# A hybrid decoder trunk on one core: a one-step mask, later conditioning products, a reordered last MLP and a last norm on VectorE

## The chip, the core and the metric

The kernel runs on one core of one Trainium2 chip. Five engines work side by side and are tied by semaphores: PE (TensorE, matrix products; PEld is its weight load), DVE (VectorE), ACT (ScalarE), POOL (GpSimd) and SP (SyncE, which here issues most transfers). SBUF is the on-chip memory, PSUM holds TensorE's sums. The metric is the device time of one execution in microseconds (us), smaller is better.

## The reference

One sequence of 256 tokens, width 1024, float32 throughout, two layers. Each layer is a mixer and an MLP, each one conditioned by shift, scale and gate computed from a vector `c`, and each closed by a layer norm.

```python
for layer in range(2):
    shift, scale, gate = ada_modulation(c, ada_w[layer, 0], ada_b[layer, 0])   # silu(c) @ w + b; 1.0 + gate
    h = x * (1.0 + scale) + shift
    y = mixer_ab(h, ...) if layer % 2 == 0 else mixer_c(h, ...)
    x = layer_norm(DN_ALPHA * x + gate * y, ln_g[layer, 0], ln_b[layer, 0])
    shift, scale, gate = ada_modulation(c, ada_w[layer, 1], ada_b[layer, 1])
    h = x * (1.0 + scale) + shift
    y = jnp.square(jax.nn.relu(h @ w1[layer])) @ w2[layer]                      # 1024 -> 4096 -> 1024
    x = layer_norm(DN_ALPHA * x + gate * y, ln_g[layer, 1], ln_b[layer, 1])
```

`mixer_ab` (layer 0) has eight heads of sliding-window attention (A) and eight heads of sparse attention (B). In B an indexer scores all earlier tokens, each query keeps the 64 with the highest scores (`lax.top_k`), and the softmax runs over these picks alone. `mixer_c` (layer 1) is block-sparse attention whose block is as long as the sequence.

## The kernel before

The 256 tokens are two blocks of 128, one token per partition; they are called block 0 and block 1. A float32 product is made of three products (lines 251 to 253): each operand is split into a high part, a cast on ScalarE (line 174), and a low part, the subtraction of that cast on VectorE or, for the weight `wo` of the mixer's output, on GpSimd (line 175). Weights come in pieces of 1 MB through four buffers that are used in turn, so that a new transfer starts when an old piece has been read.

The order on each engine comes from a list scheduler. It takes instructions in the order of the code, shifted by `later(...)` and a table `LATER` of hand-set numbers. `behind(what, m)` adds one order between two instructions: `m` comes after the instruction that was put in `state[what]` last.

The change touches four places.

*The picks of B (`select`, lines 838 to 857).* VectorE takes eight maxima eight times (lines 852, 853) and overwrites each picked score with the number `SENT`. Two instructions then make the mask: line 856 writes `NEG` (a huge negative number) where the score is not `SENT` and 0 where it is, line 857 adds the causal mask `m`. Block 0 has 128 scores per row, block 1 has 256.

*The conditioning products (`ada_product`, line 337).* A product of `c` with a 128 x 1024 piece of the conditioning weights is one VectorE instruction. Two pieces, with keys ("ada", 1, 6) and ("ada", 1, 7), that is `w_ada_1_6` and `w_ada_1_7` in the order below, are late: two products each, so four in all. They belong to the shift and the scale of layer 0's MLP. `facA` and `facB` (lines 410 to 414) are made from them.

*The attention of B (`half_step`).* TensorE makes scores (`ps_s`, line 548), VectorE their row minimum of the negated scores (`negm`, line 552), ScalarE the exponential (line 556), TensorE transposes and the product with the values (line 570), VectorE the division (lines 584, 586). In the same stretch TensorE makes the output product of the mixer (`ps_out`) into two accumulators that are used in turn, the conditioning rows (`ps_ada`, line 362), and a broadcast of the gate (line 433) from rows that ScalarE casts (line 428). `residual` (line 625) multiplies a finished accumulator by the gate and so frees it.

*The last MLP and the last norm.* The MLP goes in 16 chunks of 256 hidden columns. `first(i)` is a chunk's first layer with the activation, `second(i, b, h)` its six products into one of four accumulators (block b, half h of the 1024 columns). `finish(b, zst)` makes a block's last products and its two residuals. `held` is true for layer 0 alone: there block 1's products of chunks 13 and 14 already stand behind block 0's. The last norm of block 0 is split: 672 columns on ScalarE and GpSimd, then 352 (`beside_vector`, lines 1132 to 1143); that of block 1 is on VectorE (lines 1153 and 1155). The reciprocal root `rs` of every norm is made on GpSimd (line 317).

Of the kernel before, what the change touches and what calls it, by code (L numbers as in the profile page):

```python
# [21 lines left out]
AF = mybir.ActivationFunctionType  # L22
ALU = mybir.AluOpType

P = 128
D = 1024
KT = 8
NB = 2
# [1 line left out]
ALPHA = 4 ** 0.25  # L30
LN_EPS = 1e-5
RMS_EPS = 1e-6
NEG = -1e30
SENT = -3e38
BIG = 3e38
NTOP = 64
IW_SCALE = 8 ** -0.5 * 64 ** -0.5
# [30 lines left out]
def trunk(ctx: ExitStack, tc, c, x, pos, small, ln, ada, w_g, w_g1, w_uq, w_out, c_in, c_out, w1, w2, out):  # L68
    nc = tc.nc
# [19 lines left out]
    def col(shape, name, bufs=4, dtype=F32):  # L89
        return work.tile(shape, dtype, name=name, tag=name, bufs=bufs)  # L90
# [178 lines left out]
    xt = []  # L269
# [12 lines left out]
    for h in range(2):  # L282
        ps = pa("ps_c")
# [49 lines left out]
    def ada_product(key, j, w):  # L333

        junk = work.tile([P, D], BF16, name="junk", tag="junk", bufs=1)
        m, bias = ada_bias(key, j)
        state[key, j] = nc.vector.tensor_tensor_reduce(out=junk, in0=w, in1=cB, scale=1.0, scalar=bias,  # L337
                                                       op0=ALU.mult, op1=ALU.add, accum_out=m)
        if j == 1:
            ada_factors(key)  # L340
        return 1 - j

    def behind(what, m):

        if what in state:
            tc.add_manual_dep(m.ins, state[what].ins.name, mybir.DependencyInfo(
                mybir.DependencyClass.NoSync, mybir.DependencyReason.DATA))
# [49 lines left out]
    done = set()  # L397
# [140 lines left out]
    def drain():  # L538
        while pipe:
            advance()  # L540
# [47 lines left out]
    def together(*gens):  # L588

        gens = list(gens)  # L590
        while gens:
            for g in list(gens):
                if next(g, gens) is gens:
                    gens.remove(g)
# [24 lines left out]
    def new_z():  # L619
        return work.tile([P, D], F32, name="z", tag="w4", bufs=2), col([P, 2, 6], "stats")  # L620

    def residual(b, h, ps, gB, zst, what=None):
        z, st = zst
        s = slice(h * 512, (h + 1) * 512)
        behind(what, nc.vector.tensor_mul(z[:, s], ps, gB[:, s]))
        nc.vector.scalar_tensor_tensor(z[:, s], in0=xt[b][:, s], scalar=ALPHA, in1=z[:, s], op0=ALU.mult, op1=ALU.add)
        nc.vector.bn_stats(st[:, h], z[:, s])

    def moments(st):
        mv = col([P, 2], "mv")  # L630
# [120 lines left out]
    for b in range(NB):  # L751
# [9 lines left out]
        ps = pc("ps_cq")  # L761
# [84 lines left out]
    def select(b, sc):  # L846

        nk = P * (b + 1)
        m = mC[:, P:] if b == 0 else mC
        for r in range(NTOP // 8):  # L850
            mx = col([P, 8], "mx")
            nc.vector.max(out=mx, in_=sc[:, :nk])
            nc.vector.match_replace(out=sc[:, :nk], in_to_replace=mx, in_values=sc[:, :nk], imm_value=SENT)
            if r % 2 and r < NTOP // 8 - 1:
                yield
        nc.vector.tensor_scalar(sc[:, :nk], sc[:, :nk], -2e38, NEG, op0=ALU.is_gt, op1=ALU.mult)
        nc.vector.tensor_add(mB[:, b, :nk], sc[:, :nk], m)


    ys = [work.tile([P, D], F32, name=f"y{b}", tag="w4", bufs=2) for b in range(NB)]  # L860
# [51 lines left out]
    def mixed_out(ys, name, i, first, second, under_first, under_second, after):  # L912
# [43 lines left out]
        def go(todo):  # L956
            for group in todo.split("|"):
                for s in group.split():
                    step(s)
                yield  # L960

        together(first, go(under_first))
        together(second, go(under_second))
        drain()
        together(go(after))

# [12 lines left out]
    def mlp(l, hT, rest, rows):  # L979
# [43 lines left out]
        def second(i, b, h):  # L1023
            halves = need(("w2", l, i))
            for f in range(2):
                s = slice(f * 256 + b * P, f * 256 + (b + 1) * P)
                wh, wl = halves[f]
                o = slice(h * 512, (h + 1) * 512)
                for m in mm3(acc[b][h], (us[i][0][:, s], us[i][1][:, s]), (wh[:, o], wl[:, o]),
                             i == 0 and f == 0, i == 15 and f == 1):  # L1030
                    if held and (i > 13 or b and i == 13):
                        behind("last", m)
                        state["last"] = m

# [6 lines left out]
        for i in range(16):  # L1041
            if i >= 1:
                need(("w2", l, i - 1))
            if held and i == 15:
                need(("w2", l, i))
                ahead(2)
            if i > 1:
                first(i)
            if held and i == 15:
                for cast, low in firsts:  # L1050
                    behind("cast", cast)
                    behind("vector", low)
            if i == at:
                gB, gb = rows()
            for _ in range(steps.get(i, 0)):
                next(more)
            if i < 15:
                need(("w1", l, i + 1))
            if 1 <= i < 15:
                for b in range(NB):  # L1060
                    for h in range(2):
                        if not (held and b and i == 14):
                            second(i - 1, b, h)
        need(("w2", l, 15))

        def finish(b, zst):
            if held and b:
                for h in range(2):
                    second(13, b, h)
            if held:  # L1070
                for h in range(2):
                    second(14, b, h)
            for h in range(2):
                for i in (15,) if held else (14, 15):
                    second(i, b, h)
                residual(b, h, acc[b][h], gB, zst, "norm" if held and b else None)

        return finish, gb

# [47 lines left out]

    finish, gb = mlp(1, hT, rest, lambda: (gate_row(3), ln_rows(3)))
    zs = [new_z() for b in range(NB)]
    halves = [slice(0, 512), slice(512, D)]  # L1130

    def beside_vector(b, s, mv, rs, after=None):

        nb = col([P, 1], "nb")
        z = zs[b][0]
        nc.vector.scalar_tensor_tensor(nb, in0=mv[:, 0:1], scalar=-1.0, in1=rs, op0=ALU.mult, op1=ALU.mult)
        nc.scalar.activation(z[:, s], z[:, s], AF.Identity, bias=nb, scale=rs)
        m = nc.gpsimd.tensor_mul(xt[b][:, s], z[:, s], gb[0][:, s])
        if after:
            tc.add_manual_dep(m.ins, after.ins.name, mybir.DependencyInfo(  # L1140
                mybir.DependencyClass.NoSync, mybir.DependencyReason.DATA))
        nc.gpsimd.tensor_add(xt[b][:, s], xt[b][:, s], gb[1][:, s])
        (nc.scalar if after else nc.sync).dma_start(out[b * P:(b + 1) * P, s], xt[b][:, s])

    finish(0, zs[0])
    first = moments(zs[0][1])
    beside_vector(0, slice(0, 672), *first)
    finish(1, zs[1])
    mv, rs = moments(zs[1][1])
    beside_vector(0, slice(672, D), *first, after=state["pow"])  # L1150
    for s in halves:
        z = zs[1][0]
        nc.vector.scalar_tensor_tensor(z[:, s], in0=z[:, s], scalar=mv[:, 0:1], in1=gb[0][:, s],  # L1153
                                       op0=ALU.subtract, op1=ALU.mult)
        nc.vector.scalar_tensor_tensor(xt[1][:, s], in0=z[:, s], scalar=rs, in1=gb[1][:, s], op0=ALU.mult, op1=ALU.add)  # L1155
        nc.sync.dma_start(out[P:, s], xt[1][:, s])


def _ktiles(w, cols):
# [50 lines left out]
```

## Time and profile before

| | us |
|---|---|
| three runs | 658.65, 658.56, 656.78 |
| median | 658.56 |
| the profiled execution | 659.22 |
| its span | 657.4 |
| PE busy | 629.9 (96%) |
| DVE busy | 472.9 (72%) |
| ACT busy | 337.9 (51%) |
| POOL busy | 55.9 (9%) |

Its mean granted TensorE clock is 0.987. The span starts with the first recorded instruction and ends with the last; 1.8 us of the profiled execution lie outside it. A row of the timeline has the start in us from the span's start, the duration in us, the engine, the line, the operation, what it writes and reads with partitions x elements, a count, and in brackets the engine's idle time before it with what ended it. DMA share is the busy share of the core's 16 transfer engines.

### The profile page before, as it was taken

The numbers are of one execution on the slowest core, as the hardware profiler recorded it, in microseconds if no ns is written. First come the engines' busy times: TensorE is split into PE (matmuls) and PEld (weight loads), VectorE is DVE, ScalarE is ACT, GpSimd is POOL, SyncE is SP. The second block draws the span as 40 slices with busy tenths as digits, with TensorE's granted clock in tenths as the row PEclk, the third lists the DMA queues.
The fourth block names the chain that finished last, engine by engine and source line by source line (L and its number), as shares of the span: only waits on it lengthen the run. The fifth ranks groups of instructions, "written<-read, shape, count | busy, mean of one in ns | idle before, by whom it ended". The sixth has DMA issues, their size and how long they took to land. (4 is left out here: it accounts for less than half of the span.)

```text
span 657.4 us, 9765 instructions
## 1 busy us (share of the span) xinstructions
PE 629.9 (96%) x3762; PEld 529.9 (81%) x3762; DVE 472.9 (72%) x858; ACT 337.9 (51%) x536; POOL 55.9 (9%) x77
## 2 busy tenths in 40 slices
PE   6998998999999999999989999999999999999993
PEld 3555686878898989898877888888889899998982
DVE  2948997677788879986987985745877755553447
ACT  3315666465555445545645446855564545455440
POOL 5010147000010000200011000000000000000004
PEclk9999998999999999999989999999999999999997
DMA  8992796435789997999833683501567745665101
GB/s 311 409 415 92 279 349 257 187 128 172 276 295 331 364 348 262 373 335 372 326 129 128 231 338 137 192 1 64 192 230 274 275 182 192 223 226 192 65 0 64
DMA packets 24384, 151.50 MB, mean 230 GB/s; under 512 B 2833, under 2 KB 3089, under 8 KB 8338
## 3 DMA queue, kind: packets, MB, share of 16 engines
q1 hardware_dynamic: 24194, 150.71, 62.9%
q8 instruction: 29, 0.48, 0.3%
q10 hardware_dynamic: 144, 0.18, 0.1%
q14 instruction: 17, 0.14, 0.1%
HBM read 149.83 MB, written 1.05 MB: 229 GB/s over the span
## 5 line engine op out<-in xcount | busy, mean ns | idle before, releaser
L175 DVE TENSOR_TENSOR wl<-w_w,wh 128x1024 fp32r<-128x1024 f32 x128 | 153.5, 1222 | 76.4 <-ACT wh L174 76.2
L174 ACT CAST wh<-w_w 128x1024 fp32r<-128x1024 f32 x128 | 131.0, 1050 | 147.1 <-PE ps_m L252 67.0
L251 PE MATMUL ps_m<-hTh,wh 128*128 128x256 f32 x448 | 126.7, 283 | 0.0
L253 PE MATMUL ps_m<-hTh,wl 128*128 128x256 f32 x448 | 126.6, 283 | 0.0
L252 PE MATMUL ps_m<-hTl,wh 128*128 128x256 f32 x448 | 126.6, 283 | 0.0
L337 DVE CUSTOM_DVE_ANT_0 junk<-w_ada,cB,sm 128x1024 bf16<-128x1024 f32 x72 | 95.7, 1328 | 9.3 <-DMA w_ada<-in_ada_dram 7.9
L251 PE MATMUL ps_m<-wh,uh 128*128 128x512 f32 x256 | 101.5, 397 | 0.0
L253 PE MATMUL ps_m<-wh,ul 128*128 128x512 f32 x256 | 101.5, 397 | 0.0
L252 PE MATMUL ps_m<-wl,uh 128*128 128x512 f32 x256 | 101.0, 395 | 0.0
L252 PEld LDWEIGHTS ps_m<-hTl,wh 128*128 128x128 f32 x448 | 85.7, 191 | 1.3
L251 PEld LDWEIGHTS ps_m<-hTh,wh 128*128 128x128 f32 x448 | 85.7, 191 | 1.2
L253 PEld LDWEIGHTS ps_m<-hTh,wl 128*128 128x128 f32 x448 | 85.7, 191 | 0.1
L253 PEld LDWEIGHTS ps_m<-wh,ul 128*128 128x128 f32 x256 | 48.2, 188 | 11.3 <-DVE ul L175 0.2
L251 PEld LDWEIGHTS ps_m<-wh,uh 128*128 128x128 f32 x256 | 48.3, 189 | 10.1 <-ACT uh L174 0.3
L252 PEld LDWEIGHTS ps_m<-wl,uh 128*128 128x128 f32 x256 | 48.2, 188 | 9.7
L251 PE MATMUL ps_c<-wh,hTh 128*128 128x512 f32 x96 | 38.7, 406 | 2.1 <-ACT hTh L174 2.1
L252 PE MATMUL ps_c<-wl,hTh 128*128 128x512 f32 x96 | 38.7, 405 | 0.0
L253 PE MATMUL ps_c<-wh,hTl 128*128 128x512 f32 x96 | 38.0, 399 | 0.0
L556 ACT ACTIVATE prob<-prob,negm 128x128 f32<-128x128 f32 (+1 forms) x64 | 26.7, 451 | 18.7 <-DVE negm L552 18.7
L317 POOL TENSOR_TENSOR rs<-rs,mhalf 128x1 f32<-128x1 f32 x8 | 7.6, 944 | 330.2 <-DVE rs L633 330.2
L175 DVE TENSOR_TENSOR ul<-relu,uh 128x512 fp32r<-128x512 f32 (+1 forms) x36 | 22.6, 629 | 16.6 <-ACT uh L174 16.6
L175 DVE TENSOR_TENSOR wl<-w_ci,wh 128x1024 fp32r<-128x1024 f32 x24 | 28.8, 1221 | 5.6 <-ACT wh L174 5.6
(231 smaller groups left out, 1016.8 us busy)
## 6 DMA issues: line engine op xcount, KB each, us to landing
w_w<-in_w_dram SPq DMA_DIRECT2D x64, 1024.0 KB, 5.1
w_ada<-in_ada_dram SPq DMA_DIRECT2D x40, 1024.0 KB, 7.0
w_ci<-in_c_in_dram SPq DMA_DIRECT2D x12, 1024.0 KB, 5.7
w_ada<-in_ada_dram SPq DMA_DIRECT2D x12, 512.0 KB, 9.5
w_wo<-in_w_out_dram SPq DMA_DIRECT2D x4, 1024.0 KB, 6.0
w_co<-in_c_out_dram SPq DMA_DIRECT2D x4, 1024.0 KB, 5.1
w_g<-in_w_g_dram SPq DMA_DIRECT2D x8, 356.0 KB, 9.0
early<-in_ada_dram SPq DMA_DIRECT2D x4, 512.0 KB, 9.2
```

What stands on the lines that cost most here:

```text
L174: state["cast"] = nc.scalar.copy(dh, src)
L175: return eng.tensor_sub(dl, src, dh.bitcast(F32))
L251: return [nc.tensor.matmul(ps, a[0], b[0], start=start, stop=False), nc.tensor.matmul(ps, a[0], b[1], start=False, stop=False), nc.tensor. ...
L252: nc.tensor.matmul(ps, a[0], b[1], start=False, stop=False),
L253: nc.tensor.matmul(ps, a[1], b[0], start=False, stop=stop)]
L317: state["pow"] = nc.gpsimd.tensor_tensor(out=dst, in0=src, in1=mhalf, op=ALU.pow)
L337: state[key, j] = nc.vector.tensor_tensor_reduce(out=junk, in0=w, in1=cB, scale=1.0, scalar=bias, op0=ALU.mult, op1=ALU.add, accum_out=m)
L556: state["exp"] = nc.scalar.activation(pr[:, j, :nk], pr[:, j, :nk], AF.Exp, bias=negm[:, hd:hd + 1], scale=-1.0)
```

## The change

It has four parts.

- **A.** The two mask instructions become one, (m + SENT) − score, with `SENT` = −2e38 and `NEG` = −1e38. For a pick the score is `SENT`, and the result is the causal mask.
- **B.** The four late conditioning products are collected in `lates` and put behind the last row minimum that was recorded, the last one of block 1 in B.
- **C.** In the last MLP block 1's products of chunks 13 and 14 now also stand behind block 0's, and the first residual multiply of each half behind the statistics of the half before.
- **D.** Both blocks' last norm is on VectorE, block 0's result in pieces of 512 and 512 columns, block 1's in 512, 256 and 256, each sent off on SP's or ScalarE's queue in turn.

```diff
-NEG = -1e30
-SENT = -3e38
+NEG = -1e38
+SENT = -2e38
...
+        if key[0] == "ada" and key[1:] in ((1, 6), (1, 7)):
+            lates.append(state[key, j])
...
-    def residual(b, h, ps, gB, zst, what=None):
+    def residual(b, h, ps, gB, zst):
...
-        behind(what, nc.vector.tensor_mul(z[:, s], ps, gB[:, s]))
+        m = nc.vector.tensor_mul(z[:, s], ps, gB[:, s])
...
-        nc.vector.bn_stats(st[:, h], z[:, s])
+        return m, nc.vector.bn_stats(st[:, h], z[:, s])
...
-        nc.vector.tensor_scalar(sc[:, :nk], sc[:, :nk], -2e38, NEG, op0=ALU.is_gt, op1=ALU.mult)
-        nc.vector.tensor_add(mB[:, b, :nk], sc[:, :nk], m)
+        nc.vector.scalar_tensor_tensor(mB[:, b, :nk], in0=m, scalar=SENT, in1=sc[:, :nk], op0=ALU.add, op1=ALU.subtract)
...
+        while lates:
+            behind("least", lates.pop())
         drain()
...
-                    if held and (i > 13 or b and i == 13):
+                    if i > 13 or b and i == 13:
                         behind("last", m)
...
-                        if not (held and b and i == 14):
+                        if not (b and i == 14):
                             second(i - 1, b, h)
...
         def finish(b, zst):
-            if held and b:
+            for i in range(14 - b, 15) if held or not b else ():
                 for h in range(2):
-                    second(13, b, h)
-            if held:
-                for h in range(2):
-                    second(14, b, h)
+                    second(i, b, h)
             for h in range(2):
-                for i in (15,) if held else (14, 15):
+                for i in range(13, 16) if b and not held else (15,):
                     second(i, b, h)
-                residual(b, h, acc[b][h], gB, zst, "norm" if held and b else None)
+                m, done = residual(b, h, acc[b][h], gB, zst)
+                behind("norm" if held and b else None if held else "done", m)
+                state["done"] = done
...
-    finish(0, zs[0])
-    first = moments(zs[0][1])
-    beside_vector(0, slice(0, 672), *first)
-    finish(1, zs[1])
-    mv, rs = moments(zs[1][1])
-    beside_vector(0, slice(672, D), *first, after=state["pow"])
-    for s in halves:
-        z = zs[1][0]
-        nc.vector.scalar_tensor_tensor(z[:, s], in0=z[:, s], scalar=mv[:, 0:1], in1=gb[0][:, s],
-                                       op0=ALU.subtract, op1=ALU.mult)
-        nc.vector.scalar_tensor_tensor(xt[1][:, s], in0=z[:, s], scalar=rs, in1=gb[1][:, s], op0=ALU.mult, op1=ALU.add)
-        nc.sync.dma_start(out[P:, s], xt[1][:, s])
+        mv, rs = moments(zs[b][1])
+        for s in (slice(0, 512), slice(512, D)):
+            nc.vector.scalar_tensor_tensor(z[:, s], in0=z[:, s], scalar=mv[:, 0:1], in1=gb[0][:, s],
+                                           op0=ALU.subtract, op1=ALU.mult)
+        cuts = (0, 512, 768, D) if b else (0, 512, D)
+        for q, lo, hi in zip((nc.sync, nc.scalar, nc.sync), cuts, cuts[1:]):
+            nc.vector.scalar_tensor_tensor(xt[b][:, lo:hi], in0=z[:, lo:hi], scalar=rs, in1=gb[1][:, lo:hi],
+                                           op0=ALU.mult, op1=ALU.add)
+            q.dma_start(out[b * P:(b + 1) * P, lo:hi], xt[b][:, lo:hi])
```

What moves on the engines is seen best in their order. Lines of the changed kernel are counted anew: its 556, 588, 590 and 629 are 552, 584, 586 and 625 before. On VectorE, before, in block 1's attention of B, from the second row minimum of a pair to the first of the next pair (the numbers behind the names are the buffers'; `junk` is the discarded product of line 337, `mod1_170` its sum; `w_ada_1_6` and `w_ada_1_7` are the two late pieces; a row with one name reads out the sum or the minimum of the row ahead of it):

```order
L552 ISA prob_1137,negm_1134<-ps_s_1136,pair_370 128x256
L552 ISA negm_1134 128x1
L584 RECIPROCAL den_1151<-ps_pv_926 128x4
L337 ISA junk_1209,mod1_170<-w_ada_1_6_977,cB_123,sm_75 128x1024
L337 ISA mod1_170 128x1
L586 TENSOR_TENSOR y0_444<-ps_pv_926,den_1151 128x2x2x64
L337 ISA junk_1236,mod1_170<-w_ada_1_7_1024,cB_123,sm_75 128x1024
L337 ISA mod1_170 128x1
L552 ISA prob_1193,negm_1134<-ps_s_1192,pair_370 128x256
L552 ISA negm_1134 128x1
```

And now, behind the last row minimum of block 1, where no product stands between the minima (`yTl` is the low part of the transposed attention output, `z` the first residual):

```order
L337 ISA junk_1162,mod1_170<-w_ada_1_6_976,cB_123,sm_75 128x1024
L337 ISA mod1_170 128x1
L175 TENSOR_TENSOR yTl_985<-evac_1241,yTh_984 128x512
L588 RECIPROCAL den_1299<-ps_pv_1133 128x4
L337 ISA junk_1207,mod1_170<-w_ada_1_6_976,cB_123,sm_75 128x1024
L337 ISA mod1_170 128x1
L590 TENSOR_TENSOR y1_445<-ps_pv_1133,den_1299 128x2x2x64
L337 ISA junk_1234,mod1_170<-w_ada_1_7_1023,cB_123,sm_75 128x1024
L337 ISA mod1_170 128x1
L629 TENSOR_TENSOR z_1245<-ps_out_1079,gateB_1177 128x512
L337 ISA junk_1281,mod1_170<-w_ada_1_7_1023,cB_123,sm_75 128x1024
```

The four products have left the stretch between the row minima, and three of them stand between the last minimum and the first residual multiply; the fourth follows that multiply.

On TensorE, before, where chunk 15's first layer (`ps_m1_6075`) begins in the last MLP; the accumulators `ps_m2_4481` and `ps_m2_4482` are block 0's halves, `ps_m2_4483` and `ps_m2_4484` block 1's:

```order
L253 MATMUL ps_m2_4484<-wh_5979,ul_5932 128x512
L251 MATMUL ps_m2_4484<-wh_5983,uh_5931 128x512
L252 MATMUL ps_m2_4484<-wl_5984,uh_5931 128x512
L253 MATMUL ps_m2_4484<-wh_5983,ul_5932 128x512
L251 MATMUL ps_m1_6075<-hTh_4455,wh_5971 128x256
```

And now, where the names are two lower: `ps_m2_4479` and `ps_m2_4480` are block 0's, and `ps_m1_6061` is chunk 15's first layer:

```order
L253 MATMUL ps_m2_4480<-wh_5977,ul_5930 128x512
L251 MATMUL ps_m2_4480<-wh_5981,uh_5929 128x512
L252 MATMUL ps_m2_4480<-wl_5982,uh_5929 128x512
L253 MATMUL ps_m2_4480<-wh_5981,ul_5930 128x512
L251 MATMUL ps_m1_6061<-hTh_4453,wh_5969 128x256
```

Chunk 15's first layer now follows block 0's products of chunk 13, and block 1's twelve products of that chunk have moved behind it, to the end.

On VectorE, the end of the kernel before:

```order
L633 TENSOR_SCALAR rs_6175<-mv_6173 128x1
L625 TENSOR_TENSOR z_6141<-ps_m2_4483,gateB_5820 128x512
L1136 SCALAR_TENSOR_TENSOR nb_6178<-mv_6173,rs_6175 128x1
L1136 SCALAR_TENSOR_TENSOR nb_6219<-mv_6173,rs_6175 128x1
L626 SCALAR_TENSOR_TENSOR z_6141<-x1_81,z_6141 128x512
L627 BN_STATS stats_6142<-z_6141 128x6
```

And now:

```order
L637 TENSOR_SCALAR rs_6161<-mv_6159 128x1
L1140 SCALAR_TENSOR_TENSOR z_6125<-z_6125,mv_6159,lngB_5831 128x512 x2
L1144 SCALAR_TENSOR_TENSOR x0_79<-z_6125,rs_6161,lnbB_5832 128x512 x2
L629 TENSOR_TENSOR z_6127<-ps_m2_4481,gateB_5818 128x512
L630 SCALAR_TENSOR_TENSOR z_6127<-x1_81,z_6127 128x512
L631 BN_STATS stats_6128<-z_6127 128x6
```

Block 0's norm, four steps of 512 columns, now stands on VectorE between block 0's moments and block 1's first residual.

More of the change, by code (lines that the diff above doesn't have):

```diff
@@ L341, in ada_product @@
         return 1 - j
+    lates = []
     def behind(what, m):
@@ L1129, in trunk @@
     zs = [new_z() for b in range(NB)]
-    halves = [slice(0, 512), slice(512, D)]
-    def beside_vector(b, s, mv, rs, after=None):
-        nb = col([P, 1], "nb")
+    for b in range(NB):
+        finish(b, zs[b])
         z = zs[b][0]
[L1136 to L1143, printed above, removed]
-    finish(0, zs[0])
-    first = moments(zs[0][1])
-    beside_vector(0, slice(0, 672), *first)
-    finish(1, zs[1])
-    mv, rs = moments(zs[1][1])
-    beside_vector(0, slice(672, D), *first, after=state["pow"])
-    for s in halves:
-        z = zs[1][0]
-        nc.vector.scalar_tensor_tensor(z[:, s], in0=z[:, s], scalar=mv[:, 0:1], in1=gb[0][:, s],
-                                       op0=ALU.subtract, op1=ALU.mult)
-        nc.vector.scalar_tensor_tensor(xt[1][:, s], in0=z[:, s], scalar=rs, in1=gb[1][:, s], op0=ALU.mult, op1=ALU.add)
-        nc.sync.dma_start(out[P:, s], xt[1][:, s])
+        mv, rs = moments(zs[b][1])
[7 more added lines that the diff above has]
+            q.dma_start(out[b * P:(b + 1) * P, lo:hi], xt[b][:, lo:hi])
 def _ktiles(w, cols):
```

## The prediction

> **What bounds the kernel now.** I read the page first, to see which engine sets the time:
>
> ```profile
> span 657.4 us, 9765 instructions
> PE 629.9 (96%) x3762; PEld 529.9 (81%) x3762; DVE 472.9 (72%) x858; ACT 337.9 (51%) x536; POOL 55.9 (9%) x77
> ```
>
> TensorE is busy for 629.9 of 657.4 us, so the change can gain only where TensorE stands still, where it runs at a lower clock, or behind its last product. The second view was therefore what TensorE waited for in the stretch in which parts A and B act (82 to 130 us): two waits.
>
> ```profile
> PE ps_bc L433 <- ACT bcrows L428: 1.8, 1, 1.8
> PE ps_ada L362 <- DMA w_ada<-in_ada_dram: 1.4, 1, 1.4
> ```
>
> The third view is the table of stretches, cut at these two waits (busy time of each engine, then the granted clock, the share of the DMA engines and GB/s):
>
> ```profile
> core 0: us, PE busy (x) PEld busy (x) DVE busy (x) ACT busy (x) POOL busy (x), PEclk, DMA share, GB/s
> 82.00:98.70 16.70, 16.66 (x163) 13.57 (x162) 15.29 (x59) 11.51 (x26) 7.93 (x9) 1.00 0.96 350
> 98.70:100.06 1.36, 0.00 (x0) 0.03 (x1) 1.33 (x2) 0.00 (x0) 0.85 (x1) 1.00 1.03 416
> 110.94:112.78 1.84, 0.00 (x0) 0.02 (x1) 1.84 (x8) 1.05 (x3) 1.84 (x1) 1.00 1.01 427
> 114.45:117.87 3.42, 3.42 (x13) 2.95 (x12) 3.42 (x11) 1.95 (x4) 0.00 (x0) 0.50 0.94 333
> ```
>
> It shows a second cost that no list of waits has. After the wait of 1.84 us TensorE ran for 3.42 us, from 114.45, at a granted clock of 0.50. It issued 13 products there; at full clock that work takes about half of 3.42, so some 1.7 us went. Another such stretch, far from the change, is of the same length:
>
> ```profile
> 334.00:336.30 2.30, 0.92 (x4) 0.79 (x5) 1.97 (x4) 1.29 (x3) 0.00 (x0) 1.00 0.05 18
> 336.30:339.70 3.40, 3.40 (x10) 2.65 (x9) 3.37 (x6) 0.00 (x0) 0.00 (x0) 0.50 0.00 0
> ```
>
> It too follows a standstill, 1.38 of the 2.30 us just before it. From 114.45 to 336.30 is 221.85 us, 65 times 3.413: the clock seems to be set in steps of some 3.4 us, each by how idle the step before was. The wait at 110.94 fills half of one step.
>
> **Part A, the mask (lines 856 and 857).** Rows of VectorE, then of GpSimd in the same stretches:
>
> ```profile
> 84.54 1.99 DVE L856 TENSOR_SCALAR score<-score 128x128 f32<-128x128 f32 x1
> 87.25 0.28 DVE L857 TENSOR_TENSOR pair<-score,mC 128x128 f32<-128x128 f32 x1
> 97.73 1.98 DVE L856 TENSOR_SCALAR score<-score 128x256 f32<-128x256 f32 x1
> 99.74 0.43 DVE L857 TENSOR_TENSOR pair<-score,mC 128x256 f32<-128x256 f32 x1
> 84.08 2.37 POOL L175 TENSOR_TENSOR hTl<-w_wo,hTh 128x1024 fp32r<-128x1024 f32 x1
> 97.21 2.35 POOL L175 TENSOR_TENSOR wl<-w_wo,wh 128x1024 fp32r<-128x1024 f32 x1 [0.53 <-PE ps_s L548]
> ```
>
> Both steps of line 856 took the same 1.98 us though one is twice as wide, and each ended within 0.2 us of the subtraction on GpSimd (86.45, 99.56). They were held up by it; the work is worth 0.3 to 0.4 us. The new single instruction costs 0.28 and 0.43 by the rows of line 857 if nothing holds it, or up to 2.0 if it is held as line 856 was. VectorE wins 0.3 to 2.0 us twice. On the path that is worth nothing: up to 98.70 TensorE is busy for 16.66 of 16.70 us, and the wait that follows ends with a transfer, in a stretch in which the DMA engines are 0.96 and 1.03 busy. I take 0, with 1.4 (that whole wait) as the gain at most. If the transfers bind, a faster VectorE can't start more of them, and nothing behind it gets later, so there is no loss end.
>
> The Trainium skill ("SBUF — State Buffer", "Who interferes with whom") says that a VectorE instruction with two SBUF inputs and a GpSimd one that reads SBUF block each other, the second for the whole of the first. The new instruction has two such inputs, so by that rule it gets held like line 856, and A saves only the second instruction, 0.28 and 0.43 us. Either way the sum has 0.
>
> **Part B, the four products (line 337).** Rows of VectorE around block 1's row minima (line 552), and of the engines beside it:
>
> ```profile
> 107.91 3.39 DVE L337 CUSTOM_DVE_ANT_0 junk<-w_ada,cB,sm 128x1024 bf16<-128x1024 f32 x1
> 111.23 0.41 DVE L552 CUSTOM_DVE_ANT_0 prob<-ps_s,pair 128x256 f32<-128x256 f32 x1
> 112.01 2.58 DVE L337 CUSTOM_DVE_ANT_0 junk<-w_ada,cB,sm 128x1024 bf16<-128x1024 f32 x1
> 114.86 1.27 DVE L337 CUSTOM_DVE_ANT_0 junk<-w_ada,cB,sm 128x1024 bf16<-128x1024 f32 x1
> 116.84 1.25 DVE L337 CUSTOM_DVE_ANT_0 junk<-w_ada,cB,sm 128x1024 bf16<-128x1024 f32 x1
> 121.19 0.08 DVE L552 DVE_READ_ACCUMULATOR2_ANT negm<- 128x1 f32 x1
> 102.72 10.79 POOL L175 TENSOR_TENSOR wl<-w_wo,wh 128x1024 fp32r<-128x1024 f32 x4 [3.16 <-ACT wh L174]
> 111.68 0.91 ACT L556 ACTIVATE prob<-prob,negm 128x256 f32<-128x256 f32 x2 [2.53 <-DVE negm L552]
> 112.50 0.24 ACT L428 CAST bcrows<-ps_bt 24x128 bf16<-24x128 f32 x1
> ```
>
> The chain is plain. The first product stands ahead of a row minimum and takes 3.39 us because GpSimd's subtractions run beside it until 113.51 (without them the same product takes 1.27). ScalarE's exponential waits 2.53 us for that minimum, the cast of line 428 stands behind the exponential, and TensorE waits for the cast. With the product gone, the minimum can start at about 107.9, 3.3 us sooner. The exponential then starts near 108.8 and the cast near 110, before TensorE asks for it at 110.94. The idle of 1.84 us goes, and with it the reason for the slow step: 1.84 + 1.7 = 3.5 us. The ends for the clock term are 0 (the slow step comes for another reason) and 1.7.
>
> What is late next: the products themselves. They now run behind the last minimum, which ends at 121.27 and would end near 117.7, when GpSimd's subtractions are over, so each costs 1.27. Three of them, with the split of yT and two short steps between, put the first residual multiply at about 123. Its row, that of TensorE's product that reuses the accumulator, and a stretch of the table behind them:
>
> ```profile
> 126.10 0.69 DVE L625 TENSOR_TENSOR z<-ps_out,gateB 128x512 f32<-128x512 f32 x1 [2.15 <-PE ps_out L253]
> 129.32 0.47 PE L251 MATMUL ps_out<-wh,yTh 128*128 128x512 f32 x1
> ...
> 128.00:132.00 4.00, 4.00 (x26) 3.48 (x25) 0.86 (x3) 0.00 (x0) 0.00 (x0) 1.00 0.00 0
> ```
>
> TensorE needs that multiply done when it begins the next accumulator, now at 129.32, then at 125.8. The multiply itself waited 2.15 us for TensorE. So some 2 us of cover are left, and I cost the move at 0. The fourth product has no reader before the conditioning factors of the MLP. The transfers into the two buffers that the products free start some 5 us later. From 128 to 132 us the DMA share is 0.00, so there is room to land late; hidden.
>
> **Part C, block 1's products of chunks 13 and 14 behind block 0's.** The number of products is the same. What changes is which of ScalarE's casts wait:
>
> ```profile
> 629.75 2.00 ACT L174 CAST wh<-w_w 128x1024 fp32r<-128x1024 f32 x2 [2.13 <-PE ps_m L253]
> 638.14 0.69 DVE L175 TENSOR_TENSOR ul<-relu,uh 128x512 fp32r<-128x512 f32 x1 [4.95 <-ACT uh L174]
> ```
>
> The casts of the last weights wait for TensorE to leave a buffer. Chunk 15's first layer now runs 2.8 us sooner: 12 products pass behind it, at 0.23 to 0.24 us each, by the starts at 646.91 and 647.15 below. The casts (2.00 us for two) then wait for that first layer to leave its buffers, fall just ahead of chunk 15's activation on ScalarE, and TensorE has 12 products as cover for them. I take 0.3 us of new standstill. The ends are 0 (all covered) and 0.8 (the casts' 2.00 us and the split's 0.69 against 12 products that started a little before); there is no gain end, since no product goes away and TensorE has no wait there now.
>
> **Part D, the last norm.**
>
> ```profile
> 646.91 0.40 PE L252 MATMUL ps_m<-wl,uh 128*128 128x512 f32 x1
> 647.15 0.40 PE L253 MATMUL ps_m<-wh,ul 128*128 128x512 f32 x1
> 647.59 0.69 DVE L625 TENSOR_TENSOR z<-ps_m,gateB 128x512 f32<-128x512 f32 x1 [0.62 <-PE ps_m L253]
> 650.01 0.15 DVE L633 TENSOR_SCALAR rs<-mv 128x1 f32<-128x1 f32 x1
> 650.08 1.60 DVE L1153 SCALAR_TENSOR_TENSOR z<-z,mv,lngB 128x512 f32<-128x512 f32 x2
> 650.42 0.99 POOL L317 TENSOR_TENSOR rs<-rs,mhalf 128x1 f32<-128x1 f32 x1
> 651.39 1.07 POOL L1138 TENSOR_TENSOR x<-z,lngB 128x352 f32<-128x352 f32 x1
> 651.60 2.74 DVE L1155 SCALAR_TENSOR_TENSOR x<-z,rs,lnbB 128x512 f32<-128x512 f32 x2
> 652.53 1.25 POOL L1142 TENSOR_TENSOR x<-x,lnbB 128x352 f32<-128x352 f32 x1
> ```
>
> From the last product to line 650.08 nothing changes. The first pair then ends at 651.68 as before. Of the second pair, 2.74 us, GpSimd's two steps overlap all; without them a step of 512 takes 0.7 (half of 1.60, less a little), and 512 + 256 + 256 about 0.7 + 0.43 + 0.43 = 1.56. It starts some 0.1 sooner, since GpSimd's power step has no queue ahead. I take a gain of 1.2. The ends are 0.65 (256 columns cost as much as 512) and 1.5 (they cost the 0.28 of line 857's smaller step). The last transfer is half as large; I add nothing for it. Block 0's norm now takes four such steps, 2.9 us, on VectorE. Counted back from a last product at 647.45, block 1's 36 products take 8.4 us, so block 0's halves are complete near 638.0 and 639.4. VectorE needs 2.2 us for a half (650.01 less 647.59, without the step that joins the halves). So it is through with block 0's halves at 642.5, with its norm at 645.5 and with block 1's first half at 647.7, while the last multiply can start at 647.9. That is 0.2 us of cover; if it is gone, the end is late by what is missing, up to 0.5.
>
> **The sum.** −1.84 (idle) − 1.7 (clock) + 0 (A) + 0.3 (C) − 1.2 (D) = −4.4. The profiled execution took 659.22 us, 0.66 above the median of 658.56, so I set the sum against the middle, 658.8: 654.4 us.
>
> **The rivals.**
> 1. Only the idle goes. A slow step, here or after the standstill at 98.70, stays or appears elsewhere, because the steps lie otherwise against the idle times in another run. The three times shown, 656.78, 658.56 and 658.65, lie 1.8 apart, about one slow step. Result: 654.4 + 1.7 = 656.1. The Trainium skill ("TensorE: Matmul & The Clock Gate", "Why this matters for your kernels") allows gaps below about 3 us without a drop of the clock. By that rule a wait of 1.84 us costs 1.84 and no more. The trace has clock 0.50 right after two shorter standstills, so the rule adds little to this chance.
> 2. The front gain is hidden: TensorE, released at 110.94, soon meets another wait, say for a transfer (the DMA share is 1.01 and 0.94 in the two rows from 110.94), or the products' cover fails by 3 us. Only D's 0.9 stays: 657.8, the same.
> 3. A passes through: if a buffer is freed by VectorE and not by the transfers, the wait of 1.36 us shrinks, perhaps with a slow step behind it: 654.4 − 1.4 = 653.0, at best 651.5.
> 4. Slower: the products, now in a row behind the minimum, are held as the first one was, at 3.39 each. Then three take 10.2 us and the split of yT 1.9, and the residual multiply ends near 131.0. TensorE, which needs it at 125.8, waits 5.2 us and runs a slow step behind that, 1.7: −4.4 + 5.2 + 1.7 = +2.5, so 661.3. It decides from a multiply that ends after 130.2. It needs GpSimd busy there, and the four subtractions of its row end at 113.51.
> 5. A is no real fusion: the new step is held as long as the old one. It costs the forecast nothing.
>
> **How the numbers follow.** This kernel's runs differ by up to 0.3% without a change, so 656.6 and 660.5 bound "the same". Forecast 0.55 (653.3 to 655.6); rival 1 0.22, three in four of it below 656.6; rival 2 0.10; rival 3 0.08; rival 4 0.05. Faster 0.55 + 0.17 + 0.08 = 0.80, same 0.05 + 0.10 = 0.15, slower 0.05. The range 652.4 to 656.9 leaves out rival 4, most of rival 2 and the far end of rival 3.
>
> **What would show it.** Right: no wait of TensorE for the cast of line 428 and clock 1.00 from 104 to 125 us; the four products at about 1.27 each between 117 and 125 with no wait of TensorE for the residual; the new mask step under 1 us or as long as GpSimd beside it; no GpSimd step but the power behind 645; the last steps on VectorE at 0.7, 0.43, 0.43. Wrong: a new standstill between 110 and 140 us, a gap of over 0.8 us before the last 48 products, or VectorE still at work for block 1's first half when the last product ends.

## The result and the profile after

The changed kernel takes 654.02 us (median of six runs, 652.72 to 655.07), the kernel before 657.39 in its six runs (656.78 to 658.65). The ratio is 0.9943, 95% interval 0.9927 to 0.9958: faster by 0.4 to 0.7%, 3.4 us between the medians. The profiled execution took 655.07 us, against 659.22.

The page, and what TensorE waited for between 80 and 165 us of the changed kernel (lines are counted anew, 4 more than before):

```profile
span 653.3 us, 9761 instructions
PE 628.8 (96%) x3762; PEld 528.4 (81%) x3762; DVE 469.8 (72%) x859; ACT 336.3 (51%) x534; POOL 49.4 (8%) x73
...
PE ps_ada L366 <- DVE negm L556: 2.1, 1, 2.1
PE ps_m L251 <- ACT hTh L174: 0.9, 1, 0.9
```

The wait for the cast that the gate's broadcast needs is gone. The other one is 0.7 us longer. The list names a row minimum there that merely ended at that moment. The rows of line 366 need the transfer of conditioning piece 5: in the ten profiles that have this wait the transfer landed 0.13 to 0.14 us before these rows began (here it landed at 100.52, and they began at 100.66). The table of stretches, cut at that wait:

```profile
core 0: us, PE busy (x) PEld busy (x) DVE busy (x) ACT busy (x) POOL busy (x), PEclk, DMA share, GB/s
98.52:100.66 2.14, 0.00 (x1) 0.03 (x2) 2.14 (x7) 0.11 (x1) 0.90 (x1) 1.00 1.00 402
101.00:104.40 3.40, 3.40 (x26) 2.45 (x18) 0.94 (x6) 3.33 (x5) 2.15 (x1) 0.50 0.74 304
105.00:111.00 6.00, 6.00 (x38) 4.87 (x37) 3.03 (x12) 4.76 (x13) 6.00 (x3) 1.00 0.47 161
111.00:118.00 7.00, 7.00 (x51) 5.92 (x50) 3.97 (x14) 5.27 (x11) 1.06 (x1) 1.00 0.79 315
118.00:125.00 7.00, 7.00 (x44) 5.97 (x42) 6.55 (x13) 2.37 (x5) 0.94 (x1) 1.00 0.40 133
```

From 105 to 125 us TensorE is busy without a break at clock 1.00. The slow step behind the transfer (101.0 to 104.4) is not new. The kernel before has one in the same place, at 100.8 to 104.2, seen in this row of its table:

```profile
100.06:104.00 3.94, 3.94 (x29) 3.20 (x29) 2.35 (x14) 2.85 (x6) 1.28 (x1) 0.59 0.89 331
```

VectorE's mask steps and the four products in the changed kernel:

```profile
84.40 2.06 DVE L861 SCALAR_TENSOR_TENSOR pair<-mC,score 128x128 f32<-128x128 f32 x1
97.59 2.10 DVE L861 SCALAR_TENSOR_TENSOR pair<-mC,score 128x256 f32<-128x256 f32 x1
118.06 1.28 DVE L337 CUSTOM_DVE_ANT_0 junk<-w_ada,cB,sm 128x1024 bf16<-128x1024 f32 x1
119.96 1.25 DVE L337 CUSTOM_DVE_ANT_0 junk<-w_ada,cB,sm 128x1024 bf16<-128x1024 f32 x1
121.48 1.27 DVE L337 CUSTOM_DVE_ANT_0 junk<-w_ada,cB,sm 128x1024 bf16<-128x1024 f32 x1
123.21 0.69 DVE L629 TENSOR_TENSOR z<-ps_out,gateB 128x512 f32<-128x512 f32 x1 [0.45 <-PE ps_out L253]
123.81 1.28 DVE L337 CUSTOM_DVE_ANT_0 junk<-w_ada,cB,sm 128x1024 bf16<-128x1024 f32 x1
```

And the end of the kernel:

```profile
644.41 0.40 PE L253 MATMUL ps_m<-wh,ul 128*128 128x512 f32 x1
644.84 0.69 DVE L629 TENSOR_TENSOR z<-ps_m,gateB 128x512 f32<-128x512 f32 x1 [0.48 <-PE ps_m L253]
647.33 1.41 DVE L1140 SCALAR_TENSOR_TENSOR z<-z,mv,lngB 128x512 f32<-128x512 f32 x2
647.50 0.99 POOL L317 TENSOR_TENSOR rs<-rs,mhalf 128x1 f32<-128x1 f32 x1 [6.78 <-DVE rs L637]
648.66 1.54 DVE L1144 SCALAR_TENSOR_TENSOR x<-z,rs,lnbB 128x512 f32<-128x512 f32 x3
```

A whole run hides where time goes, since the work ahead of the change ends up to 2.6 us earlier or later from profile to profile. So I read three stages that the change and the experiments touch. *Front*: from TensorE's first row of conditioning piece 4 to the first product of layer 0's MLP. *Middle*: from layer 1's first product, 60 of its products on. *Tail*: from the 400th product before the last to the end of the span. The rows for the front, before and after:

```profile
95.49 1.07 PE L362 MATMUL ps_ada<-w_ada,cT 128*32 128x256 f32 x16
144.64 0.39 PE L251 MATMUL ps_m<-wh,hTh 128*128 128x256 f32 x1
...
95.35 1.07 PE L366 MATMUL ps_ada<-w_ada,cT 128*32 128x256 f32 x16
141.53 0.39 PE L251 MATMUL ps_m<-wh,hTh 128*128 128x256 f32 x1
```

Between front and middle, and between middle and tail, all profiles agree within 0.3 us (190.7 and 230.0 to 230.2). The stages in us, worked out in the same way from the starts in each trace (the rows below the second are the experiments, told in the next section; `pieces`, `rows_later`, `warm`, `both` and `both_warm` change the changed kernel, the others the kernel before):

| kernel | front | middle | tail | median of runs | ratio to before, 95% |
|---|---|---|---|---|---|
| before | 49.15 | 16.78 | 75.22 | | |
| changed | 46.18 | 16.82 | 74.18 | 654.02 | 0.9943 (0.9927 to 0.9958) |
| only_a | 48.11 | 15.57 | 75.21 | 656.76 | 0.9988 (0.9970 to 1.0006) |
| only_b | 46.71 | 16.76 | 75.19 | 655.34 | 0.9971 (0.9951 to 0.9991) |
| first_only | 45.59 | 16.79 | 75.21 | 654.77 | 0.9956 (0.9943 to 0.9969) |
| only_c | 49.18 | 16.79 | 75.36 | 658.03 | 1.0006 (0.9994 to 1.0018) |
| only_d | 50.09 | 16.77 | 75.06 | 657.58 | 1.0001 (0.9990 to 1.0013) |
| c_and_d | 48.43 | 15.57 | 74.13 | 656.65 | 0.9978 (0.9968 to 0.9989) |
| pieces | 50.04 | 16.80 | 74.13 | 654.75 | 0.9955 (0.9939 to 0.9970) |
| rows_later | 46.45 | 16.76 | 74.14 | 655.10 | 0.9956 (0.9943 to 0.9970) |
| fill_wait | 49.91 | 16.76 | 75.20 | 659.41 | 1.0013 (1.0002 to 1.0024) |
| warm | 45.04 | 15.56 | 74.14 | 652.16 | 0.9901 (0.9882 to 0.9920) |
| both | 45.26 | 16.77 | 74.12 | 652.93 | 0.9920 (0.9904 to 0.9935) |
| both_warm | 45.24 | 15.56 | 74.13 | 652.86 | 0.9915 (0.9893 to 0.9937) |

### The profile page after: what moved, and what is told of

Its sections match the earlier page's. It is cut to its first block, busy times and chain, and to the rows that moved or that the text cites. A ratio compares the mean times of both kernels' runs of the same rounds, so it can differ in the third digit from the quotient of the medians.

```text
span 653.3 us, 9761 instructions
## 1 busy us (share of the span) xinstructions
PE 628.8 (96%) x3762; PEld 528.4 (81%) x3762; DVE 469.8 (72%) x859; ACT 336.3 (51%) x534; POOL 49.4 (8%) x73
## 4 chain that ended last, share of the span: by engine, by line
PE 89%; DVE 4%; ACT 3%; issue 1%; DMA 1%; POOL 0%; SPq 0%; DVEq 0%; ACTq 0%
PE ps_m L251 18%; PE ps_m L253 18%; PE ps_m L252 18%; PE ps_c L252 4%; PE ps_c L251 3%; PE ps_c L253 3%; PE ps_g L684 3%; PE ps_s L552 3%; PE ps_pv L574 3%; PE ps_g L704 2%; PE ps_out L251 2%; PE ps_out L253 2%; PE ps_out L252 2%; PE ps_pt L566 2%; PE ps_ada L366 1%
## 5 line engine op out<-in xcount | busy, mean ns | idle before, releaser
L252 PE MATMUL ps_m<-wl,uh 128*128 128x512 f32 x256 | 101.0, 395 | 0.0
L337 DVE CUSTOM_DVE_ANT_0 junk<-w_ada,cB,sm 128x1024 bf16<-128x1024 f32 x72 | 92.2, 1281 | 11.3 <-DMA w_ada<-in_ada_dram 10.3
L174 ACT CAST wh<-w_ci 128x1024 fp32r<-128x1024 f32 x24 | 24.8, 1052 | 13.7 <-PE ps_c L253 9.9
```

The lines of the kernel that those rows point to most:

```text
L174: state["cast"] = nc.scalar.copy(dh, src)
L252: nc.tensor.matmul(ps, a[0], b[1], start=False, stop=False),
```

## The experiments

**The four parts one by one.** Each is the kernel before with one part of the diff shown above. Part A:

> Part A alone (the one-step mask), all else as before. Theory: the new instruction is held by GpSimd's subtraction beside it as the old one was, about 2.0 to 2.1 us each, and is hidden behind the transfer for which TensorE waits at 98.7 us. So no change, within 0.5 us of the kernel before, and the wait at 98.7 us is 1.4 us as before. Rival: the longer wait that the changed kernel shows there (2.1 us and not 1.4) comes from A; then this kernel has it too and is 0.5 to 0.8 us slower. Second rival: A passes through, 0.5 to 1.4 us faster.

Its interval holds "no change", and no gain over 0.3%. The wait at the transfer was 2.2 us in this profile, put down to the transfer by name; the next row shows the wait that B removes:

```profile
PE ps_ada L362 <- DMA w_ada<-in_ada_dram: 2.2, 1, 2.2
PE ps_bc L433 <- ACT bcrows L428: 1.1, 1, 1.1
```

So a long wait at 98.7 occurs with A, but the profiles without A have it from 0.8 (only_b) to 2.8 us (only_d) too. The landing of that transfer varies from profile to profile, so the rival, that A makes the wait longer, is not borne out.

> Part B alone (the four late products behind the last row minimum). Theory: the wait of 1.84 us at 110.94 goes and the slow clock step of 3.4 us behind it goes with it (1.7 us), less some 0.5 us lost in the new order: 2.7 to 3.2 us faster, no clock of 0.50 between 105 and 125 us. Rival: only the wait goes, a slow step stays between 105 and 125 us: 1.3 to 1.8 us faster.

Faster by 2.7 us between the medians, and no slow step after 108. The size fits the theory, the interval (0.1 to 0.5%) holds the rival's time as well.

> Part C alone (block 1's products of chunks 13 and 14 behind block 0's in the last MLP), the last norm split over ScalarE, GpSimd and VectorE as before. Theory: C by itself brings nothing and costs the 0.15 to 0.3 us of a later split of the last weights: 0 to 0.5 us slower, a gap of 0.2 to 0.5 us before the last 60 products. Rival: C is where the gain of the tail comes from; then it is 0.5 to 1.2 us faster.

> Part D alone (the last norm on VectorE), block 1's products of chunk 13 still ahead of chunk 15. Theory: D needs C. Block 0's halves are complete only near 640.1 and 641.5 us, so its norm of 2.8 us on VectorE stands in the way of block 1's first half, the last residual multiply starts 2.0 to 2.4 us later than now, and the 1.35 us gained behind it does not make up for this: 0.6 to 1.0 us slower than before. Rival: D's gain is independent of C: 1.2 to 1.4 us faster.

Both leave the time unchanged, and the tails say it more finely: C alone costs 0.14 us and D alone gains 0.16, where both together gain 1.0. VectorE's rows in D alone:

```profile
644.82 1.41 DVE L1135 SCALAR_TENSOR_TENSOR z<-z,mv,lngB 128x512 f32<-128x512 f32 x2
646.14 1.41 DVE L1139 SCALAR_TENSOR_TENSOR x<-z,rs,lnbB 128x512 f32<-128x512 f32 x2
647.47 1.28 DVE L625 TENSOR_TENSOR z<-ps_m,gateB 128x512 f32<-128x512 f32 x2
652.82 1.53 DVE L1139 SCALAR_TENSOR_TENSOR x<-z,rs,lnbB 128x512 f32<-128x512 f32 x3
```

Block 0's norm holds VectorE until 647.5. Both residual multiplies of block 1 then stand in a row (one row, x2), the first at 647.47 and not at 644.78 as before. By the starts of the next steps block 1's residuals end 1.3 us later than before, not the 2.0 to 2.4 that I had expected, and the norm behind them gains 1.4. So the delay eats the gain, and the expected loss of 0.6 to 1.0 us was too large; the rival, a gain without C, is excluded.

> Parts C and D together, without A and B. Theory: C gives D its cover. From the 400th product before the last to the end of the span the kernel before takes 75.2 us, C alone 75.4, D alone 75.1; C and D together should take 74.2 as the whole change does, so 1.0 us faster than before, with the front stage (clock 0.50 after the wait for line 428's cast) as before. Rival: the tail's gain needs the earlier start that A and B give; then it stays near 75.1 and the time is the same.

The tail is as the theory had it: 74.13 us, with a cover of 0.43 us at the last multiply, and the whole kernel 0.2% faster. The front was not as before: this profile has two slow steps in a row from 101.4 to 108.2, a wait of only 0.6 us for the cast of line 428, and no slow step behind it.

```profile
646.47 0.69 DVE L625 TENSOR_TENSOR z<-ps_m,gateB 128x512 f32<-128x512 f32 x1 [0.43 <-PE ps_m L253]
650.29 1.53 DVE L1138 SCALAR_TENSOR_TENSOR x<-z,rs,lnbB 128x512 f32<-128x512 f32 x3
...
PE ps_bc L433 <- ACT bcrows L428: 0.6, 1, 0.6
```

**Which of the four products matters.**

```diff
-        if key[0] == "ada" and key[1:] in ((1, 6), (1, 7)):
+        if key == ("ada", 1, 6) and j == 0:
             lates.append(state[key, j])
```

> The kernel before with only the first of the four late products (the one of 3.39 us at 107.91 us) put behind the last row minimum. Theory: this one product made the whole wait; the wait for line 428's cast is under 0.4 us, the stage from the rows of the sixth last conditioning piece to the MLP's first product takes 49.5 to 50.5 us and not 52.5, and the gain is that of B alone, 2 to 3 us. Rival: the remaining three, now ahead of the later minima, stop TensorE in their turn: a wait of 1 us or more for a row minimum or its exponential between 108 and 122 us, and less than half of the gain.

The question was not answered, because the engines' orders came out the same as in only_b. The likely reason is that all four products write the one `junk` buffer (line 335), so that the other three follow the first wherever it goes. The run is therefore a second measurement of B alone: 0.9956, and together with only_b a gain of 2.7 to 3.6 us.

**GpSimd's instructions in four pieces** (added to the changed kernel).

```diff
+        if eng is nc.gpsimd:
+            for o in range(0, 1024, 256):
+                m = eng.tensor_sub(dl[:, o:o + 256], src[:, o:o + 256], dh[:, o:o + 256].bitcast(F32))
+            return m
         return eng.tensor_sub(dl, src, dh.bitcast(F32))
```

> The changed kernel with each of GpSimd's subtractions for the output weights cut into four of 256 columns. Theory: VectorE's new mask step is held until the GpSimd instruction beside it ends and then runs at its own 0.3 to 0.45 us, so it takes at most 0.65 + 0.45 us, 0.4 to 1.1, and not 2.06 and 2.10. Rival: both engines share the way to memory and each is slowed in proportion; then it still takes about 2. Time: within 0.6 us of the changed kernel (it waits for a transfer), so 2.5 to 4.5 us faster than before.

```profile
84.41 0.70 DVE L865 SCALAR_TENSOR_TENSOR pair<-mC,score 128x128 f32<-128x128 f32 x1
97.60 0.48 DVE L865 SCALAR_TENSOR_TENSOR pair<-mC,score 128x256 f32<-128x256 f32 x1
97.07 3.40 POOL L177 TENSOR_TENSOR wl<-w_wo,wh 128x256 fp32r<-128x256 f32 x4 [0.19 <-PE ps_s L556]
```

The mask step takes 0.70 and 0.48 us in place of 2.06 and 2.10, at the price of a GpSimd that takes 3.40 for the subtraction that took 2.35. An instruction is held until the one beside it ends. The Trainium skill ("SBUF — State Buffer", "Who interferes with whom") has the same rule for a VectorE step with two SBUF inputs. It says more: a step with one SBUF input, outside the two-port modes, is not held. The old line 856 had one SBUF input and was held for 1.98 us; whether by such a mode, no run here shows. The time did not change: what TensorE waits for there is the transfer and not the mask step. In this profile that wait was 3.2 us and three slow steps followed it:

```profile
PE ps_ada L370 <- DMA w_ada<-in_ada_dram: 3.2, 1, 3.2
...
101.50:104.50 3.00, 2.79 (x20) 1.61 (x21) 0.00 (x0) 1.32 (x3) 3.00 (x5) 0.50 0.88 330
104.50:107.90 3.40, 3.40 (x18) 3.40 (x17) 0.67 (x5) 2.59 (x6) 3.40 (x6) 0.50 0.26 70
107.90:111.00 3.10, 3.10 (x11) 2.51 (x11) 1.30 (x5) 0.69 (x2) 1.52 (x3) 0.50 0.85 359
```

From the start of piece 5's rows to the MLP's first product this profile took 43.69 us (145.40 less 101.71), the changed kernel 40.87 (141.53 less 100.66). Two more slow steps cost 2.8 us here, by this estimate 1.4 each.

**The conditioning rows later** (the changed kernel, with a table of how many pieces go beside each half step).

```diff
-"b0": [2, 2, 0, 0]
+"b0": [2, 0, 2, 0]
```

> The changed kernel with the conditioning rows of piece 5, for whose transfer TensorE waits 1.4 to 2.1 us at 98.7, one half step of block 0's attention later. Theory: TensorE has some 1.5 us of other products ahead of that wait and waits at most 1 us there, and the slow clock step behind it goes in most runs: 1 to 2.5 us faster than the changed kernel, 4.5 to 6 faster than before. Rival: the wait only moves to the exponential behind block 0's masked minima, which the mask step holds until 99.7 us; then it is within 0.7 us of the changed kernel, and the profile shows the wait for a probability and not for a transfer.

The rival was right: the wait for the transfer is gone, one as long stands in its place, and the ratio to before (0.9956) is that of the changed kernel within the intervals.

```profile
PE ps_pt L566 <- ACT prob L560: 1.9, 1, 1.9
```

**Both together.** The diffs are the two above.

> The changed kernel with GpSimd's subtractions in four pieces and the rows of conditioning piece 5 one half step later. Theory: the mask step, now 0.5 us, lets the masked minima and their exponential end about 1 us earlier, so that the wait of 1.9 us for that exponential, which the later rows alone had, falls to 1.0 us or less, and the kernel is 0.5 to 2 us faster than the changed one, 4 to 5.5 faster than before. Rival: the split of yT (1.2 us under GpSimd), which stands ahead of the masked minima, takes the mask step's place; the wait stays at 1.3 us or more and the time within 0.5 us of the changed kernel.

Two waits for that exponential remain, 1.3 us in all and 0.8 at most, and no slow step follows in the front, which is 0.9 us shorter than the changed kernel's.

```profile
PE ps_pt L570 <- ACT prob L564: 1.3, 2, 0.8
```

At 0.9920 it is faster than the changed kernel's 0.9943 by about what was expected, though the intervals overlap. The later rows alone had 0.9956 (0.9943 to 0.9970), and the two intervals do not overlap: a shorter mask step is worth something here, where TensorE waits for what stands behind it.

**Is it the idle time that sets the clock?** Products without use were put into the waits, first into the one that B removes, in the kernel before:

```diff
             ps = pc("ps_bc")
+            for _ in range(8 if fill and h == 0 else 0):
+                nc.tensor.matmul(ps[:, 384:], ident, ident, start=True, stop=True)
```

> The kernel before with eight products without use (identity by identity, 128 x 128, into the accumulator that the gate's broadcast overwrites) ahead of the broadcast of the gate, so that TensorE works in the wait of 1.84 us for line 428's cast. Theory: the slow clock step of 3.4 us at 114.45 comes from that idle time; with work in it the clock is 1.00 from 112 to 120 us, and the kernel is 0.8 to 1.8 us faster than before though the wait itself is not shorter. Rival: the slow step has another reason; it stays, and the time is the same or up to 1 us slower for the added products.

The stretches from the added products on, and the new wait:

```profile
110.53:112.87 2.34, 2.34 (x19) 2.13 (x18) 2.34 (x8) 1.05 (x3) 2.34 (x1) 1.00 1.01 427
112.87:116.50 3.63, 3.63 (x26) 2.90 (x25) 3.59 (x6) 2.07 (x3) 0.22 (x1) 1.00 0.90 291
116.50:118.00 1.50, 0.03 (x2) 0.01 (x1) 1.50 (x10) 0.57 (x2) 0.00 (x0) 1.00 0.99 410
...
PE ps_pt L564 <- ACT prob L558: 1.5, 1, 1.5
```

The slow step is gone, as the theory said, but the time is 0.1% longer, which neither expectation had right in full. TensorE now runs at full clock into VectorE, which still has the products ahead of the row minima, and stands for 1.5 us at 116.5. (The added products also moved the fourth product ahead of a minimum, so the 1.5 us are not all due to the clock.) So the slow step may have cost little here, because VectorE was nearly as late as a slow TensorE; since the order changed too, that is not shown. Other profiles do not give a price either. From the start of piece 5's rows to the MLP's first product the kernel before took 44.58 us, this one 44.49 (144.97 less 100.48), A alone 42.79 (no slow step at 112, but a wait of 1.1 in place of 1.8) and C with D 44.19 (none at 112 either, but two at 101).

Then into the two waits that the changed kernel still has:

```diff
         ps = pa("ps_ada")
+        for _ in range(6 if key == ("ada", 1, 5) else 0):
+            in_turn(nc.tensor.matmul(ps[:, 384:], ident, ident, start=True, stop=True))
...
             ps = (pd if g == 0 and b else pa)("ps_c")
+            for _ in range(7 if (g, part, b) == (0, 0, 0) else 0):
+                nc.tensor.matmul(ps[:, 384:], ident, ident, start=True, stop=True)
```

> The changed kernel with six such products ahead of conditioning piece 5's rows (the wait for a transfer at 98.7 us) and seven ahead of layer 1's first product (the wait of 2.1 us at 330). Theory: no clock of 0.50 between 98 and 112 us nor between 330 and 338, which gives 1.7 us (one slow step) and 1.2 us: 1.5 to 3 us faster than the changed kernel, 5 to 6.5 faster than before. Rival: the slow steps stay, or the added products push the real ones back as much as they save: within 0.7 us of the changed kernel, 2.7 to 4.1 us faster than before.

```profile
97.85:99.43 1.58, 1.58 (x14) 1.39 (x13) 1.58 (x2) 0.00 (x0) 1.04 (x1) 1.00 0.99 404
99.43:100.39 0.96, 0.00 (x0) 0.00 (x0) 0.96 (x8) 0.37 (x2) 0.00 (x0) 1.00 1.10 341
100.39:104.00 3.61, 3.60 (x24) 2.59 (x28) 0.52 (x2) 2.22 (x4) 2.26 (x1) 1.00 0.66 275
330.60:334.00 3.40, 3.40 (x15) 2.78 (x16) 3.40 (x5) 0.00 (x0) 0.00 (x0) 1.00 0.00 0
```

There is no slow step from 20 to 645 us, though TensorE still stands for 0.96 and 0.55 us behind the added products. The middle takes 15.56 us and not 16.82: 1.25 us, with nothing else changed there. That is the cleanest price of a slow step that these runs have. All four runs of `warm` had a mean granted clock of 0.994 to 0.997, the six of the changed kernel 0.985 to 0.990. The front is 1.1 us shorter, but the added products also drew output products ahead of the conditioning rows, so this part is not the clock's alone. At 0.9901 (0.9882 to 0.9920) this kernel beats the changed one, whose interval begins at 0.9927.

The idle time is not the whole rule. The standstill ahead of layer 1's first product is 2.1 us in all twelve profiles without products in it. In ten of them a slow step follows. In A alone and in C with D none does, and the middle takes 15.57 us there too. Rows of A alone, then of C with D, in and behind that standstill:

```profile
331.00:332.00 1.00, 0.00 (x0) 0.00 (x0) 1.00 (x2) 0.97 (x3) 0.00 (x0) 1.00 0.20 82
334.00:335.00 1.00, 1.00 (x6) 0.82 (x5) 1.00 (x3) 0.00 (x0) 0.00 (x0) 1.00 0.00 0
...
334.00:335.00 1.00, 0.00 (x0) 0.00 (x0) 0.79 (x2) 1.00 (x2) 0.00 (x0) 1.00 0.02 8
336.00:337.00 1.00, 1.00 (x6) 0.83 (x5) 1.00 (x3) 0.00 (x0) 0.00 (x0) 1.00 0.00 0
```

Counted in steps of 3.413 us from another slow step of the same profile, the standstill lies within one step in the ten profiles. In the two others it lies across two steps: 0.4 and 1.7 us of it in A alone, 0.5 and 1.6 in C with D. So a part of what a run gains or loses is where its standstills happen to fall.

> The kernel with GpSimd's subtractions in four pieces and the rows of conditioning piece 5 one half step later, and now seven products without use ahead of layer 1's first product. Theory: the front stays as without them, the slow clock step at 330 to 334 us goes, so that the stage of 60 products of layer 1 from the first on takes 15.6 us and not 16.8: 1.0 to 1.3 us faster than that kernel, 6 to 7 us faster than before. Rival: the gain there is given back within layer 1 (a later wait for weights grows): within 0.4 us of that kernel.

The middle fell to 15.56 us as expected. The runs do not show it (652.86 against 652.93): in this profile piece 4's rows began at 96.2 us, in that of `both` at 93.6, and this spread is larger than the gain. By the stages it should be the faster; by the runs it stays open. `warm` has the lowest median of all, but the intervals of `warm`, `both` and `both_warm` overlap.

## Why the prediction was right

The time, 654.02, lies 0.4 from the forecast of 654.4, and the sign and the mechanism hold. The gain was smaller than forecast: 3.4 us and not 4.4. The three runs shown had a median of 658.56; six have 657.39. My starting point was 1.4 too high, and that made up for a sum that was 1.0 larger than this gain. That the time came out within 0.4 is thus luck in part. The interval of the ratio, 2.8 to 4.8 us, holds both gains, so the runs do not show the sum to be too large.

- *A, 0.* Right. The new step was held for the full length (2.06, 2.10), the upper end of the price. The transfer that hides it was itself 0.7 us later in the profiled execution, which no term had.
- *B, idle, −1.84, and clock, −1.7.* Right in the profiled pair: the row minimum starts at once, and the wait and the slow step behind it are gone. From the start of piece 5's rows to the MLP's first product TensorE took 44.58 us before (144.64 less 100.06) and 40.87 after: 3.7 less, where the two terms make 3.54. The front as a whole gained 2.97, because the wait for the transfer ahead of those rows was 0.73 longer. The runs of B alone gave 2.7 and 3.6. The weak point of the sum is that it took both terms from one execution. Of the five profiles without B or added products, the kernel before and C alone have a wait of 1.8 us with a slow step behind it. A alone has a wait of 1.1 us and C with D one of 0.6, both without a slow step behind it, and D alone, with its three slow steps ahead, has no wait there. What B takes away differs between executions, and no run shows its mean for each term. Where a slow step could be priced, it cost 1.25 us (layer 1) and, by an estimate, 1.4 (`pieces`), less than the 1.7 that I had; behind this wait it could not be priced by itself. Rival 1 looked for a slow step that stays. One does, at 101 us, but the kernel before has it too, so it costs no difference.
- *The products' cover.* Right: 1.25 to 1.28 us each, the multiply at 123.21 where I had about 123, and it waited 0.45 us for TensorE. Rival 4 had no footing, with GpSimd done by 112.
- *C, +0.3.* Right: the last 400 products took 0.37 us more (65.30 against 64.93).
- *D, −1.2.* A little small: from the last multiply to VectorE's end 5.36 us and not 6.75, so 1.39. The first pair of norm steps became faster too (1.41 for 1.60), which I had left as it was. The cover of 0.2 was 0.48.

The Trainium skill's bound on gaps ("TensorE: Matmul & The Clock Gate", "Why this matters for your kernels": no more than about 3 us) did not hold: gaps of 1.4 to 2.2 us were followed by clock 0.50 in most profiles, one of 1.1 us (C with D, at 99.1) too, and none was in the three profiles with added products in the gap. Gaps of 1.5 (`fill_wait`), 1.1 (A alone) and 0.96 us (`warm`) were not followed by it, nor were the two of 2.1 us that lay across two steps.

## What to carry to other kernels

Price a wait of the bound engine together with what it triggers, but see in several profiles whether the wait and its slow clock are there at all: here the wait that B removes was 1.8, 1.1, 0.6 us or none. Then ask which engine is next late, since it can take back what the faster clock gives. Moving a slow step off one engine needs its cover in the order of another; here the last norm on VectorE was worth 0.2 us without the reordered products and 1.0 with them. And where runs differ by more than the gain, compare stages between two fixed instructions. The tail repeats to 0.06 us among profiles with the same code there, where whole runs differ by three. The front, which holds the wait for a transfer, differs by 1.1 us between `only_b` and `first_only`, whose orders are the same.

## What the runs showed of the hardware

A standstill of TensorE of 1.4 to 2.2 us was followed by one slow step of 3.4 us in most profiles, one of 1.1 us by two in a row (C with D), and one of 2.8 (D alone) or 3.2 us (`pieces`) by three in a row, although TensorE was busy for nearly all of that time. The same standstill of 2.1 us was not followed by one where it lay across two steps. A slow step cost 1.25 us at the start of layer 1 and, by an estimate, 1.4 in the front of `pieces`. With work without use in the gap no slow step followed, in any of the three profiles. How much work a step must hold to keep the clock up was not measured: 1.7 us of idle time in one step passed in A alone, 1.4 did not in the kernel before.
